# Two more seven-product tiles in the second group's feed-forward, with the first group's last sums done among them

## The chip, the cores and the metric

The kernel runs on one core of a Trainium2 chip. The metric is the device time of one execution in microseconds; the median of a few executions is given. The core has a matrix engine (TensorE, PE in the profile), a vector engine (VectorE, DVE), a scalar engine (ScalarE, ACT), a general engine (GpSimd, POOL), and a queue engine that only issues transfers (SyncE, SP).

## What is computed

One layer of a streaming encoder, for a prompt of 1024 frames and 32 frames of a running stream, with the same weights. The first half (three kinds of mixing heads, an output projection, a layer norm) is left out here, since the change doesn't touch it. The second half is a gated feed-forward with a residual and a layer norm:

```python
    mix = jnp.concatenate([...], axis=-1) @ w_o
    x = _layer_norm(ALPHA * x + (1 + g1) * mix, ln1_g, ln1_b)
    h = x * (1 + sc2) + sh2
    y = (jax.nn.silu(h @ w_gate) * (h @ w_up)) @ w_down
    x = _layer_norm(ALPHA * x + (1 + g2) * y, ln2_g, ln2_b)
```

The model width is 1024, the hidden width of the feed-forward 2816, that is 22 tiles of 128 columns.

## The kernel before

**Layout.** Activations lie with the feature on the partitions: 8 tiles (k) of 128 features by the frames. The 1056 frames are two groups: group 0 has 512 frames, group 1 has 544 (512 of the prompt's second half and the 32 others), worked on in two ranges of 272 columns. All matrix products are made in three matmuls of a rounded type, high part by high part, high by low and low by high (`gemm`, lines 130 to 132), so each operand is split first: ScalarE rounds it (the cast that makes `whi`, `ah`, `acth`), VectorE subtracts to get the rest (`wlo`, `al`, `actl`). For weights that is `weights` (lines 117 and 118).

**Order of the work around the change.** Group 0's feed-forward comes first. The 22 tiles j of gate and up weights are cut into six lists (`GROUPS`); after the tiles of a list and one more, `down` adds that list's share of the down projection into `z`. In the last list of group 0 (`g == WOB`) group 1's output projection and its first layer norm (`ln1`, phase `lna1`) are woven in. That norm writes group 1's modulated input `h` in two parts as the operand of the next products (`hh`, `hl`, lines 1240 and 1241) and also stores it to memory (`self.dh`, line 1239). Then comes the last `down` of group 0, whose evacuation (line 1212) is followed by `ln_sum` for group 0's second norm: a square on ScalarE (line 1073), a running sum of squares on VectorE (line 1074, `qs`) and a running sum on GpSimd (line 1083, `zs`), 16 pieces of 256 columns. `ln1_res(1)` turns group 1's normed rows into the residual of its second norm: 16 in-place scalings on GpSimd (line 1268). They must be done before group 1's first `down` adds to `z`.

**Group 1's tiles.** Tiles 0, 1 and 2 go by `up`: gate and up product, each for two ranges, each 8 k by 3 matmuls: 96 matmuls of 272 columns. From tile 3 (`SJ = 3`) on, `sup` makes the same 2 x 2 blocks (gate and up; first and second half of k; two ranges) by seven block products in the manner of Strassen and Winograd: 7 x 4 k x 3 = 84 matmuls. It needs sums of weight blocks and sums of operand blocks.

- The weights: per tile, three loads (gate weights, a part of the weight sums `self.dp[j]`, and 256 KB of the up weights called `w2`), then two adds on VectorE (lines 1387 and 1388) and splits of `w1`, `w3`, `w4` (128x1024 each) and `w2` (128x512) at lines 1381 and 1382. `self.dp[j]` is made in memory by `sums`: a copying transfer from SP's queue (line 1331) and an accumulating transfer from GpSimd's queue (line 1333), a few tiles ahead.
- The operand: `sup_operand` loads `h` from `self.dh`, k and k + 4 together, makes four sums of 272 columns (lines 1356 to 1359) and splits two rows of 544 (lines 1361 and 1362) into `self.T`, which lies where group 0's operand lay (`ah`, `al` of the pool `ph`). Four steps k. Its buffers hold two steps; the loads of the next two are issued after the step whose buffers they take.
- The products of a tile stand in the order: 1 and 2 on `w1` with the plain operand, 3 on `w3` with T's first part, 4 on `w4` with T, 5 on `w3` with the plain operand, 6 on `w4` and 7 on `w2` with T. Lines 1407 to 1411, 1418 and 1419 take them out of PSUM; lines 1413 to 1422 make the gated activation and split it.

The steps of the operand are issued while `up` of tiles 0 to 2 is written, behind the last activation (`lastact`). Behind every tile from 3 on, `turns` gives a number of steps of group 0's second norm (`ln2`, phase `lnb0`): first the mean and variance, then per k a subtraction (line 1465), a scaling (line 1481), an affine step on ScalarE (line 1483) and, for every second k, a store.

Each engine runs its instructions in one fixed order, which a planner makes from the order in which the program writes them and from estimated times; `issue_after` holds an instruction behind another one in that plan.

Of the kernel before, what the change touches and what calls it, by code (L numbers as in the profile page):

```python
# [7 lines left out]
F32 = mybir.dt.float32  # L8
# [7 lines left out]
P = 128  # L16
# [30 lines left out]
FF = 22  # L47
SJ = 3
TS = 1
# [19 lines left out]
class Kernel:  # L69
    def __init__(self, ctx, tc, d):  # L70
        self.ctx, self.tc, self.nc, self.d = ctx, tc, tc.nc, d
        self.n = 0
        self.phase = "start"

    def pool(self, name, bufs=1, ctx=None, **kw):
# [22 lines left out]
    def tie(self, ins, target, engines):  # L98
        for i in ins:
            if i.engine in engines and "DMA" not in type(i).__name__ and "Dma" not in type(i).__name__:  # L100
                self.tc.add_manual_dep(i, target.ins.name, mybir.DependencyInfo(
                    mybir.DependencyClass.NoSync, mybir.DependencyReason.SCHED_ONLY), reason="order")

    def weights(self, src, nk, ncol, eng=None, pool=None):
# [958 lines left out]
    def ln_sum(self, st, z, m, sl):  # L1063
# [5 lines left out]
        if st["last"] and m != o[7]:  # L1069
            sq = self.t((self.pg, self.pu)[m % 2], [P, 512], F32, self.utag[m % 2])[:, :sl.stop - sl.start]  # L1070
        else:
            sq = self.t(self.p2, [P, 272], F32, "tmp", 4)[:, :sl.stop - sl.start]
        nc.scalar.activation(sq, z[:, m, sl], AF.Square)
# [260 lines left out]

    def sup_operand(self, ks):

# [6 lines left out]
        def load(k):  # L1343
            self.phase = "sup"
            x, y = ((self.t(self.px, [P, 544], F32, z, 1) for z in ("c", "uv")) if k % 2 else
                    (f(self.t(self.px, [P, 544], F32R, z, 1)) for z in ("w2h", "w2l")))
            self.load(x, self.dh[:, k])
            self.load(y, self.dh[:, k + 4])
            return x, y

        loaded = {k: load(k) for k in ks[:2]}
        yield
        for k in ks:
# [6 lines left out]
            for z, (h, l) in zip((x, y), self.T):  # L1360
                nc.scalar.copy(h[:, k], z)
                tt(l[:, k], z, f(h[:, k]), ALU.subtract)
            if k + 2 in ks:
                loaded[k + 2] = load(k + 2)
            yield
# [218 lines left out]
    def run(self):  # L1584
# [164 lines left out]
        for g, (j0, nj) in enumerate(GROUPS):  # L1749
# [26 lines left out]
            for j in range(j0 + (g > 0), j0 + nj + (g < last)):  # L1776
                weave(self.up(0, j, act, pa, WIDE if 0 < j < GROUPS[-1][0] else MM[0]))
            if g == WOB - 1:
                st = self.ln_begin(nc.gpsimd, sum=False)
                self.down(0, g, act, WIDE, st)  # L1780
            else:
                self.down(0, g, act, WIDE)
        st.update(pivot=False, sum=True)
        self.down(0, last, act, MM[0], st)
        self.ln1_res(1)
        self.st0 = st
# [3 lines left out]
        self.px = self.pool("px")  # L1790
        operand = self.sup_operand(range(4))
        next(operand)
# [5 lines left out]
        norm0 = norm0()  # L1798
        turns = [1, 1, 2, 2, 2, 1] * 2
        for g, (j0, nj) in enumerate(GROUPS):  # L1800
            for j in range(j0 + (g > 0), min(j0 + nj + (g < last), FF - TS)):
                if self.nsum <= FF:
                    self.sums()
                if j >= SJ:
                    self.sup(j, act, pa)
                    with tc.issue_after(self.lastact.ins):
                        for _ in range(turns.pop(0) if turns else 0):
                            next(norm0, None)
                    continue
                for i, _ in enumerate(self.up(1, j, act, pa, MM[1])):  # L1810
                    if 0 < 2 * j + i // 2 < 5 and i % 2:
                        with tc.issue_after(self.lastact.ins):
                            next(operand, None)
            if g < last:
# [135 lines left out]
```

## Time and profile before

| what | us |
|---|---|
| median of 3 executions | 1334.85 |
| lowest, highest | 1334.41, 1336.23 |
| the profiled execution | 1335.24 |
| its span, first to last instruction | 1333.1 |

The profile is of one execution, so its own time, 1335.24, belongs to its rows; 2.1 us lie around the span. Engines are named PE, DVE, ACT, POOL and SP; PEld is the loading of weights into the matrix engine. A row of the timeline has the start, the time taken, engine, line of the kernel, operation, output <- inputs, shape, and in square brackets the idle time before it with what ended it. Tiles are named by the phase that made them, so a buffer taken over from an earlier phase can carry that one's name. Rows with "x14 | 9.2, 707" are groups: count, busy time in us, mean in ns.

### The profile page before, as it was taken

The page shows a single profiled execution, that of the slowest core. Times are in us where ns is not written, and L with a number is a line of the kernel's source. Part 1 is how long each engine was busy: PE and PEld are TensorE (multiplying, and loading weights), DVE is VectorE, ACT ScalarE, POOL GpSimd, SP SyncE. Part 2 cuts the span into 40 slices and gives each one's busy share as a digit, 9 for nine tenths or more (in the row PEclk, how much of TensorE's full clock was granted, in tenths as well). Part 3 has the DMA queues.
Part 4 walks back from the last instruction along what each step waited for, and adds up shares of the span by engine and source line. Part 5 has one row for each costly group of instructions (what it writes and reads, how often), then busy time and mean ns, then how long its engine had stood idle before and what let it go on. Part 6 is the DMA issues. An engine that isn't in the chain of part 4 may idle for free.

```text
span 1333.1 us, 24982 instructions
## 1 busy us (share of the span) xinstructions
PE 1318.8 (99%) x9426; PEld 1197.1 (90%) x9426; DVE 989.8 (74%) x2106; ACT 648.3 (49%) x1285; POOL 183.0 (14%) x219
## 2 busy tenths in 40 slices
PE   9999999999999999999999999999999999999996
PEld 6798888978999888888887888999999999999996
DVE  5636667667778677777776676778989997978677
ACT  3424446444437645455355354436664463635344
POOL 0102100011305000000000001134700000000523
PEclk9999999999999999999999999999999999999998
DMA  9775565533758755354343333663786866644311
GB/s 365 279 257 167 177 181 180 153 129 111 223 170 257 186 137 147 112 163 115 112 137 111 102 104 125 194 159 114 207 216 166 233 185 181 183 134 140 98 49 67
DMA packets 118119, 217.43 MB, mean 163 GB/s; under 512 B 18324, under 2 KB 62480, under 8 KB 118000
## 3 DMA queue, kind: packets, MB, share of 16 engines
q1 hardware_dynamic: 111184, 204.37, 48.8%
q0 software_dynamic: 5616, 10.86, 4.9%
q8 instruction: 74, 1.21, 0.4%
q10 hardware_dynamic: 1200, 0.62, 0.2%
q14 instruction: 45, 0.37, 0.1%
HBM read 184.95 MB, written 50.77 MB: 177 GB/s over the span
## 4 chain that ended last, share of the span: by engine, by line
PE 96%; DMA 1%; ACT 1%; SPq 0%; DVE 0%; issue 0%; ACTq 0%
PE up_g L132 6%; PE up_g L130 6%; PE up_g L131 6%; PE dn_g L132 4%; PE dn_g L130 4%; PE dn_g L131 4%; PE tm_g L404 4%; PE tm_g L406 3%; PE tm_g L405 3%; PE sup_u L132 3%; PE sup_u L131 3%; PE sup_u L130 3%; PE fox_t L938 2%; PE wo_g L130 2%; PE wo_g L132 2%; PE wo_g L131 2%
## 5 line engine op out<-in xcount | busy, mean ns | idle before, releaser
L131 PE MATMUL up_g<-ada_al,up_whi 128*128 128x512 f32 (+1 forms) x384 | 140.5, 366 | 0.0
L132 PE MATMUL up_g<-ada_ah,up_wlo 128*128 128x512 f32 (+1 forms) x384 | 140.3, 365 | 0.0
L130 PE MATMUL up_g<-ada_ah,up_whi 128*128 128x512 f32 (+1 forms) x384 | 140.1, 365 | 0.0
L1381 ACT CAST sup_whi<-sup_raw 128x1024 fp32r<-128x1024 f32 x54 | 56.6, 1051 | 96.7 <-PE dn_u L131 39.9
L117 ACT CAST up_whi<-up_raw 128x1024 fp32r<-128x1024 f32 x50 | 52.5, 1049 | 68.0 <-PE dn_g L131 35.8
L130 PEld LDWEIGHTS up_g<-ada_ah,up_whi 128*128 128x128 f32 x384 | 72.4, 189 | 11.5 <-issue 0.4
L131 PEld LDWEIGHTS up_g<-ada_al,up_whi 128*128 128x128 f32 x384 | 72.4, 189 | 11.0
L132 PEld LDWEIGHTS up_g<-ada_ah,up_wlo 128*128 128x128 f32 x384 | 72.5, 189 | 10.7
L1382 DVE TENSOR_TENSOR sup_wlo<-sup_raw,sup_whi 128x1024 fp32r<-128x1024 f32 x54 | 69.1, 1280 | 15.3 <-ACT sup_whi L1381 15.3
L1212 DVE SCALAR_TENSOR_TENSOR wo_z<-dn_g,start_mod,wo_z 128x512 f32<-128x512 f32 (+4 forms) x120 | 60.2, 521 | 22.7 <-PE dn_g L132 22.3
L911 ACT ACTIVATE fox_p<-fox_s,fox_fmx 128x384 f32<-128x384 f32 (+2 forms) x96 | 55.1, 578 | 45.1 <-DVE fox_fmx L909 25.4
L130 PE MATMUL dn_g<-up_acth,dn_whi 128*128 128x512 f32 (+2 forms) x200 | 73.7, 370 | 0.0
L132 PE MATMUL dn_g<-up_acth,dn_wlo 128*128 128x512 f32 (+2 forms) x200 | 73.7, 368 | 0.0
L131 PE MATMUL dn_g<-up_actl,dn_whi 128*128 128x512 f32 (+2 forms) x200 | 73.4, 368 | 0.0
L118 DVE TENSOR_TENSOR up_wlo<-up_raw,up_whi 128x1024 fp32r<-128x1024 f32 x50 | 64.6, 1293 | 8.6 <-ACT up_whi L117 7.7
L906 DVE TENSOR_REDUCE fox_fmx<-fox_s 128x1 f32<-128x384 f32 (+2 forms) x96 | 53.1, 554 | 21.1 <-PE fox_s L903 19.8
L117 ACT CAST dn_whi<-dn_raw 128x1024 fp32r<-128x1024 f32 (+1 forms) x44 | 42.7, 971 | 49.5 <-PE up_g L131 33.3
L943 ACT CAST fox_pth<-fox_t 128x512 fp32r<-128x512 f32 (+1 forms) x80 | 41.6, 542 | 43.1 <-PE fox_t L938 42.1
L118 DVE TENSOR_TENSOR dn_wlo<-dn_raw,dn_whi 128x1024 fp32r<-128x1024 f32 (+1 forms) x44 | 49.5, 1126 | 9.8 <-ACT dn_whi L117 9.7
L944 DVE TENSOR_TENSOR fox_ptl<-fox_t,fox_pth 128x512 fp32r<-128x512 f32 (+1 forms) x80 | 49.8, 632 | 7.0 <-ACT fox_pth L943 6.7
L1333 POOL DMA_DIRECT2D start_dp<-w_gu x19 | 19.7, 1039 | 226.0 <-DMA start_dp<-w_gu 226.0
L404 PE MATMUL tm_g<-tm_whi,start_ah 128*128 128x264 f32 (+2 forms) x160 | 49.9, 312 | 0.0
(694 smaller groups left out, 4680.6 us busy)
## 6 DMA issues: line engine op xcount, KB each, us to landing
up_raw<-w_gu SPq DMA_DIRECT2D x50, 512.0 KB
ada_late<-w_ada SPq DMA_DIRECT2D x28, 512.0 KB
dn_raw<-w_dn SPq DMA_DIRECT2D x28, 512.0 KB
sup_raw<-w_gu SPq DMA_DIRECT2D x20, 512.0 KB
start_dp<-w_gu SPq DMA_DIRECT2D x19, 512.0 KB
start_dp<-w_gu POOLq DMA_DIRECT2D x19, 512.0 KB, 8.6
wo_raw<-w_o SPq DMA_DIRECT2D x18, 512.0 KB
sup_raw<-start_dp SPq DMA_DIRECT2D x18, 512.0 KB
```

Of the source, the lines that this page charges most:

```text
L117: nc.scalar.copy(hi[:, :w], raw[:, :w])
L118: (eng or nc.vector).tensor_tensor(lo[:, :w], raw[:, :w], f(hi[:, :w]), ALU.subtract)
L130: nc.tensor.matmul(ps, hi, xh(k), start=start and k == 0, stop=False)
L131: nc.tensor.matmul(ps, hi, xl(k), start=False, stop=False)
L132: self.lastmm = nc.tensor.matmul(ps, lo, xh(k), start=False, stop=stop and k == n - 1)
L404: nc.tensor.matmul(ps[:, :ncol], xh, hi, start=k == 0, stop=False)
L906: nc.vector.tensor_reduce(mxs[:, x:x + 1], s[:, :w], AX.X, ALU.max, negate=True)
L911: nc.scalar.activation(pr[:, lo:hi], banks[x][:, :hi - lo], AF.Exp, bias=mxs[:, 0:1], accum_out=sums[:, x:x + 1])
L944: nc.vector.tensor_tensor(pl[:, :e], ps[:, :e], f(ph[:, :e]), ALU.subtract)
L1212: self.lastz = self.nc.vector.scalar_tensor_tensor(z[:, m, x:y], ps[:, x - a:y - a], g[i], z[:, m, x:y], ALU.mult, ALU.add)
L1381: nc.scalar.copy(h, x)
L1382: tt(l, x, f(h), ALU.subtract)
```

## The change

Group 1's tiles 1 and 2 go by `sup`, too (`SJ = 1`). So two more weight sums are made in memory: `sums` runs after tiles 17 and 18 of group 0 as well, and from there on makes the sums of the same tiles at the same places as before.

The operand T is thus needed after tile 0. All eight loads are issued at the start: step 2 and 3 are loaded into two of the five buffers of `acth` and `actl`. The four steps are written between the parts of tile 0, without being held behind the last activation.

`ln_sum` for group 0's second norm is no longer done in the last `down` but behind tiles 2, 3, 4 and 5, four pieces each (`SUMS`), ahead of the norm's turns; the square has a buffer of its own. `ln1_res(1)` is written after tile 0. All GpSimd instructions of both get a dependency on the last subtraction of the operand (`behind`). The turns of the norm stand behind the same tiles as before up to tile 8, then start again at tile 11.

```diff
-SJ = 3
+SJ = 1
+TURNS = (0, 0, 1, 1, 2, 2, 2, 1)
+SUMS = (0, 4, 4, 4, 4)
...
+    def behind(self, first):
+
+        for i in self.nc.cur_bb.bb.instructions[first:]:
+            if i.engine == mybir.EngineType.Pool:
+                self.tc.add_manual_dep(i, self.lastT.ins.name, mybir.DependencyInfo(
+                    mybir.DependencyClass.Sync, mybir.DependencyReason.DATA), reason="behind")
...
-            sq = self.t(self.p2, [P, 272], F32, "tmp", 4)[:, :sl.stop - sl.start]
+            pool, w, tag, n = (self.px, 256, "sq", 1) if st is self.st0 else (self.p2, 272, "tmp", 4)
+            sq = self.t(pool, [P, w], F32, tag, n)[:, :sl.stop - sl.start]
...
-            x, y = ((self.t(self.px, [P, 544], F32, z, 1) for z in ("c", "uv")) if k % 2 else
+            x, y = ((self.t(self.px, [P, 544], F32, z, 1) for z in ("c", "uv")) if k == 1 else
+                    (f(self.t(pool, [P, 544], F32R, z, 5)) for z in ("acth", "actl")) if k else
                     (f(self.t(self.px, [P, 544], F32R, z, 1)) for z in ("w2h", "w2l")))
...
-        loaded = {k: load(k) for k in ks[:2]}
+        loaded = {k: load(k) for k in ks}
...
-                tt(l[:, k], z, f(h[:, k]), ALU.subtract)
-            if k + 2 in ks:
-                loaded[k + 2] = load(k + 2)
+                self.lastT = tt(l[:, k], z, f(h[:, k]), ALU.subtract)
...
                 weave(self.up(0, j, act, pa, WIDE if 0 < j < GROUPS[-1][0] else MM[0]))
+                if j > GROUPS[-1][0] - 2:
+                    self.sums()
...
-        st.update(pivot=False, sum=True)
+        st.update(pivot=False)
         self.down(0, last, act, MM[0], st)
-        self.ln1_res(1)
         self.st0 = st
...
-        turns = [1, 1, 2, 2, 2, 1] * 2
+
+        def sum0():
+            for a, b in MM[0]:
+                for m in range(KT):
+                    self.phase = "dn0"
+                    first = len(nc.cur_bb.bb.instructions)
+                    self.ln_sum(self.st0, self.z[0], m, slice(a, b))
+                    self.behind(first)
+                    yield
+
+        sum0 = sum0()
+        sums = list(SUMS)
+        turns = list(TURNS) * 2
...
                     with tc.issue_after(self.lastact.ins):
+                        for _ in range(sums.pop(0) if sums else 0):
+                            next(sum0, None)
                         for _ in range(turns.pop(0) if turns else 0):
                             next(norm0, None)
...
                 for i, _ in enumerate(self.up(1, j, act, pa, MM[1])):
-                    if 0 < 2 * j + i // 2 < 5 and i % 2:
-                        with tc.issue_after(self.lastact.ins):
-                            next(operand, None)
+                    next(operand, None)
+                if j == 0:
+                    for _ in operand:
+                        pass
+                    first = len(nc.cur_bb.bb.instructions)
+                    self.ln1_res(1)
+                    self.behind(first)
```

More of the change, by code (lines that the diff above doesn't have):

```diff
@@ L73, in __init__ @@
         self.phase = "start"
+        self.st0 = None
     def pool(self, name, bufs=1, ctx=None, **kw):
@@ L1333, in sums, with sup_operand @@
             self.nc.gpsimd.dma_start(self.dp[i - 1], blocks(i - 1)[:, 0:4:3], accum_op=ALU.add)
-    def sup_operand(self, ks):
+    def sup_operand(self, ks, pool):
         nc = self.nc
@@ L1790, in run @@
         self.px = self.pool("px")
-        operand = self.sup_operand(range(4))
+        operand = self.sup_operand(range(4), pa)
         next(operand)
```

## The prediction

> **What bounds the kernel now.** I read the page first: engine shares, then the chain that ended last.
>
> ```profile
> span 1333.1 us, 24982 instructions
> PE 1318.8 (99%) x9426; PEld 1197.1 (90%) x9426; DVE 989.8 (74%) x2106; ACT 648.3 (49%) x1285; POOL 183.0 (14%) x219
> PE 96%; DMA 1%; ACT 1%; SPq 0%; DVE 0%; issue 0%; ACTq 0%
> ```
>
> TensorE is busy for 99% of the span and is 96% of the chain, so a matmul taken out is worth its pitch, as long as nothing else becomes late. The share of VectorE, 74%, is an average, so I read the stretch that the change touches. First the timeline of TensorE, at the first matmul of group 1's tiles 0, 1, 2, of tile 3 (the first by seven products), and of what follows it:
>
> ```profile
> 946.09 0.28 PE L130 MATMUL up_g<-wo_ah,up_whi 128*128 128x272 f32 x1
> 958.10 0.29 PE L130 MATMUL up_g<-wo_ah,up_whi 128*128 128x272 f32 x1
> 970.13 0.29 PE L130 MATMUL up_g<-wo_ah,up_whi 128*128 128x272 f32 x1
> 982.16 0.29 PE L130 MATMUL sup_u<-wo_ah,sup_whi 128*128 128x272 f32 x1
> 992.68 0.38 PE L1095 MATMUL lnb_t<-up_zs,start_onesm 128*128 128x256 f32 x1
> ```
>
> A plain tile takes 12.03 us (96 matmuls, 0.125 us each), a seven-product tile 10.52 us (84 matmuls). Then the windows view around it: the end of group 1's first norm; from there to the end of group 1's first down projection; tiles 4 to 6 with the second.
>
> ```profile
> core 0: us, PE busy (x) PEld busy (x) DVE busy (x) ACT busy (x) POOL busy (x), PEclk, DMA share, GB/s
> 928.33:952.22 23.89, 23.89 (x203) 23.89 (x201) 23.82 (x45) 13.88 (x31) 19.51 (x19) 1.00 0.52 156
> 952.22:1011.80 59.58, 59.58 (x473) 59.32 (x472) 54.72 (x106) 34.33 (x67) 9.77 (x12) 1.00 0.86 222
> 1011.80:1061.80 50.00, 50.00 (x402) 50.00 (x401) 45.60 (x88) 25.06 (x37) 4.10 (x4) 1.00 0.72 194
> ```
>
> TensorE never stops, but VectorE has 0.07 us, then 4.9 us, then 4.4 us to spare. It is the next bound, and the change gives it more to do.
>
> **The change part by part.**
>
> *Matmuls removed.* Two tiles lose 12 matmuls each: 2 x (12.03 - 10.52) = **3.0 us**, all on the path. This is the whole possible gain, and it is certain.
>
> *VectorE, per tile.* One run without gaps in the VectorE timeline gives the pitch (start to start) of each operation of a seven-product tile:
>
> ```profile
> 1021.67 0.72 DVE L1418 TENSOR_TENSOR sup_c<-sup_g,sup_uv 128x544 f32<-128x544 f32 x1
> 1022.30 1.22 DVE L1382 TENSOR_TENSOR sup_wlo<-sup_raw,sup_whi 128x1024 fp32r<-128x1024 f32 x1
> 1023.44 0.43 DVE L1419 TENSOR_TENSOR sup_c<-sup_u,sup_c 128x272 f32<-128x272 f32 x1
> ...
> 1029.04 0.72 DVE L1422 TENSOR_TENSOR sup_actl<-sup_c,sup_acth 128x544 fp32r<-128x544 f32 x1
> 1029.67 0.42 DVE L1465 TENSOR_TENSOR wo_z<-wo_z,up_zs 128x256 f32<-128x256 f32 x1
> 1030.05 0.44 DVE L1411 TENSOR_TENSOR sup_sil<-sup_u,sup_uv 128x272 f32<-128x272 f32 x1
> 1030.41 0.42 DVE L1481 TENSOR_TENSOR wo_z<-wo_z,up_pv 128x256 f32<-128x256 f32 x1
> ```
>
> From 1021.67 to 1029.67 stand 13 of a tile's 15 operations, 8.0 us; the third large split (1.14) and L1411 (0.36) make 9.5 us. A plain tile has two such splits and six 272-wide operations: 2 x 1.14 + 6 x 0.36 = 4.4 us. Two tiles add 2 x 5.1 = 10.2 us of VectorE.
>
> *VectorE, what is freed.* Three things move: the 16 residual scalings on GpSimd go behind the last operand subtraction; group 0's 16 squares (ScalarE), 14 adds on VectorE and 14 on GpSimd go behind tiles 2 to 5. Before, they share the time of the norm:
>
> ```profile
> 949.86 1.75 DVE L118 TENSOR_TENSOR up_wlo<-up_raw,up_whi 128x1024 fp32r<-128x1024 f32 x1
> 952.22 5.55 DVE L1074 TENSOR_TENSOR up_qs<-up_qs,dn_tmp 128x256 f32<-128x256 f32 x4
> L1074 DVE TENSOR_TENSOR up_qs<-up_qs,dn_tmp x14: 407/413/4331, 951.5 to 961.4; 128x256 f32<-128x256 f32 x14
> L1074 DVE TENSOR_TENSOR up_qs<-up_qs,dn_tmp 128x256 f32<-128x256 f32 x14 | 9.2, 707 | 0.0
> 953.13 1.22 POOL L1083 TENSOR_TENSOR up_zs<-up_zs,wo_z 128x256 f32<-128x256 f32 x1
> 955.66 1.15 POOL L1083 TENSOR_TENSOR up_zs<-up_zs,wo_z 128x256 f32<-128x256 f32 x1
> L1268 POOL TENSOR_SCALAR wo_z<-wo_z,start_colp 128x272 f32<-128x272 f32 x8 | 9.3, 1167 | 0.4 <-ACT lna_tmp L1236 0.4
> 944.95 0.47 DVE L1212 SCALAR_TENSOR_TENSOR wo_z<-dn_u,start_mod,wo_z 128x256 f32<-128x256 f32 x1
> 945.34 0.47 DVE L1212 SCALAR_TENSOR_TENSOR wo_z<-dn_g,start_mod,wo_z 128x256 f32<-128x256 f32 x1
> ```
>
> While GpSimd runs, a split takes 1.75 instead of 1.22 us, and one add of 0.41 us took 4.33 us, beside GpSimd operations that stand back to back around 953 to 957. Of the 45 VectorE instructions from 928.33 to 952.22, 4 are splits, 14 are L1212 (pitch 0.39), some 27 are 256 or 272 wide: 4.6 + 5.5 + 9.7 = 19.8 us of work in 23.9 us. So 4.1 us are lost there, and 3.9 us more in the one long add. Two GpSimd adds of the norm itself (L1233) stay, so I choose to count 3.0 us of the 4.1 as won: the norm's last subtraction ends at 949.2 instead of 952.2.
>
> *The sum for VectorE* up to the end of the first down projection, in place of 54.72 us: minus tile 1's evacuation (2.2) and tile 2's all (4.4), minus the adds (9.2, 0.4 of it before 952.22: 8.8), plus the 8 of them that come back behind tiles 2 and 3 (2.9), plus two tiles (19.0), minus the 2.3 us that fit into tile 1's old split slots: **58.9 us**. There are 949.2 to 1008.8 (1011.8 less 3.0), 59.6 us. Bounds of what that costs: nothing, since TensorE never waited at 23.82 of 23.89 us; or, if VectorE keeps half of its 4.9 us of idle time and the moved GpSimd work costs it 1.5 us again (the 4.1 us above, less the norm's own, cut to half), 58.9 + 2.4 + 1.5 - 59.6 = 3.2 us. I take the middle, **1.6 us**.
>
> *The operand (T).* It is now due in tile 1. One k in the VectorE timeline:
>
> ```profile
> 965.32 0.43 DVE L1356 TENSOR_TENSOR sup_w2l<-sup_w2l,sup_w2h 128x272 f32<-128x272 f32 x1
> 965.79 0.44 DVE L1357 TENSOR_TENSOR sup_w2h<-sup_w2h 128x272 f32<-128x272 f32 x1
> ...
> 967.10 0.43 DVE L1312 TENSOR_TENSOR up_sil<-up_g,up_sil 128x272 f32<-128x272 f32 x1
> 967.45 0.72 DVE L1362 TENSOR_TENSOR lna_al<-sup_w2h,lna_ah 128x544 fp32r<-128x544 f32 x1
> 968.09 0.72 DVE L1362 TENSOR_TENSOR lna_al<-sup_w2l,lna_ah 128x544 fp32r<-128x544 f32 x1
> 968.72 0.43 DVE L1313 TENSOR_TENSOR up_sil<-up_u,up_sil 128x272 f32<-128x272 f32 x1
> ```
>
> 3.4 us less the foreign L1312 (0.35) is 3.05 us; with other work in the gaps of the dependent ones (0.47 against 0.36) 2.7. Product 3 starts two products (3.0 us) after 958.1, and reaches its fourth k at 962.2. VectorE from 949.2: rest of the sum weights 1.8, operand 10.4 to 11.6 (four k's, the last subtraction not needed yet), one evacuation 1.1: 962.5 to 963.7, so 0.3 to 1.5 us late. This is the same lateness seen at its first place, not added to 1.6.
>
> *Waits added.* GpSimd's scalings wait for the last operand subtraction; behind them in its queue stand the accumulating DMA issues, whose sums are used several tiles later, and the adds. 16 x 1.17 = 18.7 us from 963.7 end at 982.4, and the first down projection, which reads them, starts after 990. The squares have one buffer, so ScalarE waits for each add, with weight casts behind it; at 34.33 of 59.58 us it has room.
>
> *DMAs.* Eight operand loads instead of four stand at the head of SP's queue, and wait for the norm's stores:
>
> ```profile
> 949.09 0.86 SPq L90 DMA_DIRECT2D start_dh<-lna_tmp  x2
> 952.28 0.42 ACT L1073 ACTIVATE dn_tmp<-wo_z 128x256 f32<-128x256 f32 x1 [2.16 <-DMA start_dh<-lna_tmp]
> 780.00:815.00 35.00, 35.00 (x228) 31.66 (x227) 24.14 (x48) 19.74 (x42) 0.00 (x0) 1.00 0.26 85
> ```
>
> A store lands about 3 us after its issue; a load of that length brings the last k at 956, in time. Two more weight sums (four DMAs of 512 KB) are issued earlier, where the DMA engines are 26% busy: nothing. Two more w2 loads, 0.5 MB at 222 GB/s, are 2.4 us of transfer in a stretch at 86%, used last in their tiles: nothing, or part of the 3.2.
>
> *Later.* Tiles 4 and 5 get 8 adds (2.9 us): 48.5 of 50 us, no wait. The norm's turns fall on the same tiles as before.
>
> **Sum:** 1335.24 (span 1333.1 and 2.1 around it) - 3.0 + 1.6 = 1333.84. That execution is 0.39 above the median shown, so against 1334.85 I say **1333.5 us**.
>
> **The rivals.**
> *Full gain.* VectorE packs as densely as from 928 to 952 and TensorE waits for nothing: 1334.85 - 3.0 = 1331.9. For it: no wait of TensorE anywhere in the stretch before. Against it: 99% of VectorE's time is asked for.
> *GpSimd collides again.* The moved 16 scalings and 14 adds meet the splits and sums of tiles 1 to 3, where VectorE has no slack, and cost what they cost before, 4.1 + 3.9 = 8.0 us: 1334.85 - 3.0 + 8.0 = 1339.9. It decides from 5.7 us of lost time on. For it: the 4.33 us add. Against it: the operand is kept clear of it, and the scalings spread.
> [...]
> *Operand loads late.* If store and load each took the 8.6 us that the accumulating DMAs take,
>
> ```profile
> start_dp<-w_gu POOLq DMA_DIRECT2D x19, 512.0 KB, 8.6
> ```
>
> the last k comes at 949.6 + 17.2 + 2.4 = 969.2, 7 us late: 1338.9.
> That the change doesn't do what it says can't be: the matmuls are gone, and the wait on GpSimd is written as a dependency.
>
> **How the numbers follow.** A measurement of this kernel can tell about 0.2%, 2.7 us, from no change: 1332.2 to 1337.5. Forecast (TensorE loses 0.4 to 5.6 us of 3.0): 0.57. Full gain: 0.24. Collision: 0.13. Loads: 0.06. So faster 0.24, same 0.57, slower 0.19. The range, 1331.6 to 1338.3, leaves out most of the collision and the loads; the forecast's own is 1332.2 to 1335.1 (1.6 replaced by 0.4 and 3.2).
>
> **What would show it.** Tiles 1 and 2 at 84 matmuls; first matmul of tile 3 at 979.2 plus what was lost. Right: a wait of TensorE of 0.3 to 1.5 us at product 3 of tile 1 on L1362, and VectorE over 97% busy from 949 to 1008. Wrong: VectorE idle there by over 3 us with no wait of TensorE (full gain), or VectorE operations of 1.7 us and more beside L1268 (collision), or L1356 of the last k waiting for a DMA after 958 (loads).

## The result, and the profile after

| | us | executions |
|---|---|---|
| before | 1334.63 (1334.03 to 1336.23) | 4 |
| after | 1349.18 (1347.92 to 1349.94) | 4 |
| ratio | 1.0104 (95%: 1.0092 to 1.0117) | |
| profiled execution after, its span | 1349.14, 1347.2 | 1 |

The change makes the kernel 1% slower, by 14.5 us. The prediction was 1333.5, no difference that can be measured, in a range of 1331.6 to 1338.3: the time lies 11 us above the range.

Lines of the changed file stand 10 to 12 further down: L130 is now L140, L1074 L1085, L1083 L1094, L1095 L1106, L1268 L1279, L1333 L1344, L1356 L1368, L1362 L1374, L1382 L1392. In the runs from e8 on, many stand 3 further still; e10 has the lines of before. First the page after: span, busy time, and the shares of the chain that ended last.

```profile
span 1347.2 us, 24929 instructions
PE 1320.5 (98%) x9402; PEld 1197.3 (89%) x9402; DVE 994.5 (74%) x2120; ACT 652.4 (48%) x1283; POOL 185.0 (14%) x221
PE 88%; DMA 4%; DVE 3%; POOL 2%; ACT 1%; issue 1%; SPq 0%; DVEq 0%; ACTq 0%; POOLq 0%
```

TensorE's share of the chain fell from 96% to 88%, and the chain now passes through DMA, VectorE and GpSimd: the end is set elsewhere for a while. Where, the waits of TensorE say (waiting instruction, what released it, total, times, longest):

```profile
PE lnb_t L1106 <- POOL up_zs L1094: 10.2, 1, 10.2
...
PE sup_u L141 <- DVE dn_al L1374: 1.1, 1, 1.1
PE wo_g L141 <- DVE up_al L1164: 0.7, 2, 0.4
...
PE sup_g L140 <- ACT sup_whi L1391: 0.4, 1, 0.4
```

None of these four stood in the profile before. One makes most of the loss: `lnb_t` at L1106, the matmul that takes the mean of group 0's second norm, waits 10.2 us for GpSimd's running sum `zs`. GpSimd's timeline there, and TensorE's row:

```profile
971.76 1.04 POOL L1344 DMA_DIRECT2D start_dp<-w_gu  x1 [10.17 <-DMA start_dp<-w_gu]
972.38 20.14 POOL L1279 TENSOR_SCALAR wo_z<-wo_z,start_colp 128x272 f32<-128x272 f32 x16
992.49 2.60 POOL L1094 TENSOR_TENSOR up_zs<-wo_z 128x256 f32<-128x256 f32 x2
995.06 10.04 POOL L1094 TENSOR_TENSOR up_zs<-up_zs,wo_z 128x256 f32<-128x256 f32 x12
```
```profile
1004.47 1.22 PE L1106 MATMUL lnb_t<-up_zs,start_onesm 128*128 128x256 f32 x2 [10.18 <-POOL up_zs L1094]
```

The 16 residual scalings wait for the last operand subtraction and start at 972.38. Behind them, in order, stand the 14 adds of `zs`: 20.14 + 2.60 + 10.04 us, to 1005. TensorE works in order too: the mean's matmuls stand right behind tile 3, which ends at 994.3, and the next product behind them; it is busy 0.00 of the 10.17 us from 994.30 to 1004.47. It waits for a sum that needs no hurry. The mean's matmul takes one half of 256 columns, seven of the 14 adds. But the first two adds, which read no `zs`, begin the two halves, so the halves are interleaved, and the wait ends only where the last add begins.

The stop costs more than its length. Windows around it (busy time of PE, PEld, DVE, ACT, POOL, then the granted clock, DMA share, GB/s):

```profile
994.00:1000.00 6.00, 0.29 (x3) 0.07 (x1) 6.00 (x8) 1.17 (x2) 6.00 (x6) 0.93 0.98 320
1000.00:1004.50 4.50, 0.03 (x1) 0.03 (x1) 0.83 (x2) 0.00 (x0) 4.50 (x8) 0.50 0.58 215
1004.50:1010.00 5.50, 5.50 (x24) 5.32 (x25) 0.72 (x1) 2.91 (x6) 3.66 (x4) 0.55 0.60 82
1010.00:1016.00 6.00, 6.00 (x50) 6.00 (x49) 4.71 (x11) 2.02 (x3) 0.00 (x0) 1.00 1.09 185
```

After the stop TensorE runs 5.5 us at a granted clock of 0.55 and only then at 1.00: 5.5 x 0.45 = 2.5 us of full clock are missing, and the section behind the stop is 1.7 us longer than before, though two of its four mean matmuls have moved out of it. In finer windows the clock is 1.00 until 999.0, some 5 us into the stop, 0.50 from 999.5 on, and 1.00 again from 1009.5, some 5 us behind the stop.

The rest is smaller. From the first matmul of each section in TensorE's timeline, before and after:

| section | before | after | difference |
|---|---|---|---|
| up to group 1's output projection | 850.15 | 850.51 | +0.36 |
| output projection | 49.03 | 50.40 | +1.37 |
| group 0's last tiles and down projection, with group 1's norm | 46.91 | 47.21 | +0.30 |
| tile 0 | 12.01 | 12.03 | +0.02 |
| tiles 1 to 3 | 34.58 | 34.14 | -0.44 (-3.01 of matmuls, +2.57) |
| stop at the mean | 0 | 10.18 | +10.18 |
| mean and first down projection | 19.12 | 20.79 | +1.67 |
| tiles 4 to 6 | 31.58 | 32.45 | +0.87 (matmuls of the norm moved here) |
| from there to the end of the span | 289.72 | 289.49 | -0.23 |

The sum is 14.10, the difference of the spans (1347.2 - 1333.1). The matmuls are gone, as forecast; the upstream 1.4 us come from transfers. SyncE's rows and GpSimd's after, then the windows before and after:

```profile
831.59 0.44 SPq L89 DMA_DIRECT2D sup_w<-w_gu  x1
832.07 0.60 SPq L93 DMA_DIRECT2D start_dp<-w_gu  x1
```
```profile
839.47 1.04 POOL L1344 DMA_DIRECT2D start_dp<-w_gu  x1 [0.64 <-DMA start_dp<-w_gu]
```
```profile
835.00:850.00 15.00, 15.00 (x112) 14.27 (x111) 10.33 (x18) 5.65 (x14) 3.06 (x3) 1.00 0.57 174
```
```profile
835.00:850.00 15.00, 15.00 (x110) 14.19 (x109) 9.55 (x15) 4.14 (x9) 4.38 (x4) 1.00 0.87 239
```

One weight sum more (a copy at 832, its accumulation at 839) lies beside the loads of group 1's mix and brings the DMA share from 0.57 to 0.87; the output projection then waits for its operand (`wo_g` in the waits). The difference in tiles 1 to 3 is 1.07 us at the operand and 0.4 at a weight split, with some more in pieces too short for the list of waits.

### The profile page after: what moved, and what is told of

The parts are those of the page before. It is cut to its first block, busy times and chain, and to the rows that moved or that the text cites. A ratio compares the mean times of both kernels' runs of the same rounds, so it can differ in the third digit from the quotient of the medians.

```text
span 1347.2 us, 24929 instructions
## 1 busy us (share of the span) xinstructions
PE 1320.5 (98%) x9402; PEld 1197.3 (89%) x9402; DVE 994.5 (74%) x2120; ACT 652.4 (48%) x1283; POOL 185.0 (14%) x221
## 4 chain that ended last, share of the span: by engine, by line
PE 88%; DMA 4%; DVE 3%; POOL 2%; ACT 1%; issue 1%; SPq 0%; DVEq 0%; ACTq 0%; POOLq 0%
PE up_g L142 6%; PE up_g L140 6%; PE up_g L141 6%; PE dn_g L142 4%; PE dn_g L140 4%; PE dn_g L141 4%; PE tm_g L414 3%; PE tm_g L416 3%; PE tm_g L415 3%; PE sup_u L142 3%; PE sup_u L141 3%; PE sup_u L140 3%; PE fox_t L948 2%; PE wo_g L141 2%; PE wo_g L142 2%; PE wo_g L140 2%
## 5 line engine op out<-in xcount | busy, mean ns | idle before, releaser
L140 PE MATMUL up_g<-ada_ah,up_whi 128*128 128x512 f32 (+1 forms) x384 | 140.1, 365 | 0.0
L1391 ACT CAST sup_whi<-sup_raw 128x1024 fp32r<-128x1024 f32 x60 | 62.4, 1049 | 87.1 <-PE dn_u L141 38.4
L1392 DVE TENSOR_TENSOR sup_wlo<-sup_raw,sup_whi 128x1024 fp32r<-128x1024 f32 x60 | 76.2, 1275 | 11.1 <-ACT sup_whi L1391 11.0
L140 PEld LDWEIGHTS up_g<-ada_ah,up_whi 128*128 128x128 f32 x384 | 72.4, 189 | 11.5 <-ACT fm_qkh L487 0.4
L127 ACT CAST up_whi<-up_raw 128x1024 fp32r<-128x1024 f32 x46 | 48.3, 1051 | 66.8 <-PE dn_g L141 35.8
L142 PE MATMUL dn_g<-up_acth,dn_wlo 128*128 128x512 f32 (+2 forms) x184 | 69.3, 377 | 0.0
L140 PE MATMUL dn_g<-up_acth,dn_whi 128*128 128x512 f32 (+2 forms) x184 | 69.0, 376 | 0.0
L141 PE MATMUL dn_g<-up_actl,dn_whi 128*128 128x512 f32 (+2 forms) x184 | 69.0, 376 | 0.0
L128 DVE TENSOR_TENSOR up_wlo<-up_raw,up_whi 128x1024 fp32r<-128x1024 f32 x46 | 59.3, 1289 | 9.1 <-ACT up_whi L127 8.1
L1344 POOL DMA_DIRECT2D start_dp<-w_gu x21 | 21.8, 1103 | 306.7 <-DMA start_dp<-w_gu 306.7
```

Of the source, the lines that this page charges most:

```text
L127: nc.scalar.copy(hi[:, :w], raw[:, :w])
L128: (eng or nc.vector).tensor_tensor(lo[:, :w], raw[:, :w], f(hi[:, :w]), ALU.subtract)
L140: nc.tensor.matmul(ps, hi, xh(k), start=start and k == 0, stop=False)
L141: nc.tensor.matmul(ps, hi, xl(k), start=False, stop=False)
L142: self.lastmm = nc.tensor.matmul(ps, lo, xh(k), start=False, stop=stop and k == n - 1)
L1391: nc.scalar.copy(h, x)
```

## The experiments

Four theories were tried. **A**: GpSimd's order makes the loss (mean behind adds behind scalings); take the wait and the slow clock behind it away, and some 1336.5 us are left. **B**: VectorE is too full, and the time is lost whatever stands on GpSimd. Two came up on the way. **C**: GpSimd's adds, once they run back to back, shut VectorE out. **D**: the additional weight sums delay group 1's output projection. Each run has its ratio to runs of the kernel before on the same chip; before lay at 1334.2 to 1335.6.

| run | tiles by seven from | median (lowest to highest), executions | ratio, 95% |
|---|---|---|---|
| e1 mean later | 1 | 1342.34 (1337.95 to 1349.80), 8 | 1.0057, 1.0034 to 1.0081 |
| e2 scalings early | 1 | 1341.08 (1339.25 to 1347.54), 7 | 1.0059, 1.0037 to 1.0080 |
| e3 seven alone | 1 | 1344.64 (1343.69 to 1345.85), 4 | 1.0068, 1.0051 to 1.0085 |
| e4 later alone | 3 | 1344.96 (1343.91 to 1345.58), 4 | 1.0072, 1.0057 to 1.0087 |
| e5 weight sums later | 1 | 1345.49 (1338.67 to 1348.85), 4 | 1.0079, 1.0050 to 1.0108 |
| e6 scalings on ScalarE | 1 | 1346.58 (1346.01 to 1348.29), 4 | 1.0096, 1.0081 to 1.0111 |
| e7 no GpSimd | 1 | 1338.93 (1338.10 to 1340.35), 6 | 1.0036, 1.0024 to 1.0049 |
| e8 spread | 1 | 1337.52 (1336.07 to 1338.70), 8 | 1.0024, 1.0013 to 1.0034 |
| e9 two with spread | 2 | 1336.13 (1334.34 to 1340.15), 11 | 1.0012, 1.0003 to 1.0020 |
| e10 two alone | 2 | 1337.24 (1336.50 to 1339.45), 11 | 1.0020, 1.0010 to 1.0029 |
| e11 two early | 2 | 1336.34 (1335.01 to 1339.31), 11 | 1.0013, 1.0004 to 1.0023 |
| e12 three early | 1 | 1337.90 (1335.37 to 1340.13), 9 | 1.0023, 1.0013 to 1.0033 |
| e13 two held | 2 | 1334.17 (1332.90 to 1335.79), 11 | 0.9996, 0.9987 to 1.0005 |
| e14 three held | 1 | 1343.99 (1343.01 to 1346.01), 5 | 1.0069, 1.0055 to 1.0083 |
| e15 three, not held | 1 | 1339.76 (1338.57 to 1343.08), 5 | 1.0042, 1.0028 to 1.0055 |

**e1, the mean later.** The norm's turns start one tile later, and its matmuls may not pass ahead of a tile's last matmul.

```diff
-TURNS = (0, 0, 1, 1, 2, 2, 2, 1)
+TURNS = (0, 0, 0, 1, 1, 2, 2, 2, 1)
...
-        turns = list(TURNS) * 2
+        turns = list(TURNS) + [1, 1, 2, 2, 2, 1]
...
+                            self.tie(nc.cur_bb.bb.instructions[first:], self.lastmm, (mybir.EngineType.PE,))
```

> The mean of group 0's second norm is written behind tile 4 instead of tile 3, and its matmul is held behind tile 4's last product on TensorE; all else is as in the changed kernel. Theory A (TensorE stops at that one matmul, for sums that stand behind 16 scalings on GpSimd): the wait of 10.2 us goes and with it the 2.5 us that the lowered clock took behind it, so 1349.2 - 12.7 = 1336.5, between 1335.5 and 1338. Theory B (VectorE can't supply two more seven-product tiles, and the one long wait only covers that): TensorE waits for VectorE or ScalarE in tiles 3 to 6 instead, 1341 or more.

The wait of 10.2 us is gone; no wait of TensorE behind the start is over 1.5 us. The fastest executions (1337.95, 1338.41) are near A, but the eight scatter over 12 us, and their mean granted clock falls with the time, 0.998 to 0.990. The profiled one, 1342.57, takes 51.04 us in the output projection and 15.45 in tile 1, and no VectorE operation there is over 1.5 us. A names the stop rightly and isn't all.

**e2, the scalings early.** `ln1_res(1)` goes back to its place in the kernel before, with no wait.

```diff
         self.down(0, last, act, MM[0], st)
+        self.ln1_res(1)
...
-                    self.ln1_res(1)
-                    self.behind(first)
```

> The 16 residual scalings on GpSimd go back to where they were before the change, without the wait for the operand; the 14 adds on GpSimd keep it. Theory A: the adds start at the last operand subtraction (about 972, or a few us later since the scalings now slow the norm's VectorE work) and need 12.6 us, so the sums are there at 985 to 989; the mean's matmul stands in tile 3 and waits 0 to 4 us: 1336 to 1341. Theory B: no change to speak of against the changed kernel, 1346 to 1350.

The wait at the mean shrinks to 0.3 us. The executions fall into two groups, 1339.25 to 1341.08 and 1347.20 to 1347.54. The same program differs by 6 to 8 us from one execution to another: something is left to chance.

**e3, the seven products alone.** The sums, squares and scalings stand as in the kernel before; only tiles 1 and 2 change.

```diff
-SUMS = (0, 4, 4, 4, 4)
+SUMS = ()
...
-        st.update(pivot=False)
+        st.update(pivot=False, sum=True)
         self.down(0, last, act, MM[0], st)
+        self.ln1_res(1)
```

> Tiles 1 and 2 by seven products alone: the sums, the squares and the scalings of group 0 stay in its last down projection, as before the change. Theory A: no long wait at the mean, since its sums are made early; 3.0 us of matmuls are gone, and the operand comes later than in the changed kernel, because GpSimd slows the norm (3 us) and the adds stand on VectorE ahead of it: TensorE waits 3 to 7 us for it in tile 1: 1334.6 - 3.0 + 3 to 7 = 1334.6 to 1338.6. Theory B: VectorE is fuller still than in the changed kernel, 1349 or more.

9 us over before, with no GpSimd work moved; 2.2 of it stand in the output projection (51.18). TensorE's waits and two windows:

```profile
PE sup_u L141 <- DVE lna_al L1374: 4.7, 2, 2.5
PE sup_u L140 <- DVE up_sil L1324: 2.0, 1, 2.0
```
```profile
970.00:976.00 6.00, 2.36 (x13) 2.14 (x14) 6.00 (x13) 3.14 (x7) 0.00 (x0) 0.75 0.28 85
976.00:982.00 6.00, 6.00 (x36) 6.00 (x36) 6.00 (x15) 0.96 (x4) 1.03 (x1) 0.68 0.42 122
```

With the sums in the way TensorE stops 6.7 us in tile 1, 4.7 of it at the operand, and the granted clock is 0.75 in 970 to 976 and 0.68 in 976 to 982; in e2, where only the sums are moved away, it stops 1.8 us. So moving the sums away was needed; moving them cost something else.

**e4, the moved sums alone.** Tiles 1 and 2 stay plain.

```diff
-SJ = 1
-TURNS = (0, 0, 1, 1, 2, 2, 2, 1)
-SUMS = (0, 4, 4, 4, 4)
+SJ = 3
+TURNS = (1, 1, 2, 2, 2, 1)
+SUMS = (8, 4, 4)
...
-                if j > GROUPS[-1][0] - 2:
-                    self.sums()
```

> The later sums and scalings alone: tiles 1 and 2 go by plain products as before the change (no weight sums for them), the operand is made in tile 0 with all its loads ahead, and 8 of the pieces stand before the norm's first turn behind tile 3, 4 and 4 behind tiles 4 and 5. Theory A: the same long wait though VectorE has 10 us less to do: scalings and adds need 20 + 13 us from the last operand subtraction, 965 to 970, so the mean's matmul, at about 993, waits 5 to 10 us, and the clock is lowered behind it for 1 to 3 us: 1341 to 1347. Theory B: VectorE has room, no wait: 1334 to 1336.

Also 9 us over before, and in A's range, but not by A's path: the wait at the mean is 2.4 us, not 5 to 10. 4.1 us are lost in tile 0 (16.07 us, before 12.01), where TensorE waits 2.48 us for a rest of the norm that stands in VectorE's order behind the operand's first load. And 1.5 us are a wait at the down projection, behind one long operation. VectorE's timeline, and GpSimd's beside it:

```profile
990.24 11.51 DVE L128 TENSOR_TENSOR dn_wlo<-dn_raw,dn_whi 128x768 fp32r<-128x768 f32 x1 [0.23 <-ACT dn_whi L127]
```
```profile
990.36 1.43 POOL L1094 TENSOR_TENSOR up_zs<-wo_z 128x256 f32<-128x256 f32 x2
991.74 7.62 POOL L1094 TENSOR_TENSOR up_zs<-up_zs,wo_z 128x256 f32<-128x256 f32 x11
999.31 0.83 POOL L1344 DMA_DIRECT2D start_dp<-w_gu  x1
999.91 1.00 POOL L1094 TENSOR_TENSOR up_zs<-up_zs,wo_z 128x256 f32<-128x256 f32 x1
```

A split of 128x768, 0.95 us elsewhere, takes 11.51 us, from the first of GpSimd's 14 adds to past the last one, with one DMA issue among them. That is C, though here little of it is on the path. The output projection takes 49.03 us, as before, with no additional weight sum: D.

**e5, the weight sums later.** e1, and the sums after tiles 17 and 18 are made where the first one is.

```diff
-                self.sums()
+                for _ in range(3):
+                    self.sums()
...
-                if j > GROUPS[-1][0] - 2:
-                    self.sums()
```

> The kernel of the run with the later mean, with one thing more: the two added weight sums are not started behind tiles 17 and 18 of group 0, but together with the first of the others, behind group 1's output projection. Theory D (the early transfers delay the loads of that projection): group 0's next products start at 899.2 to 899.6, as before the change, instead of 902.1; the fastest runs get 2 to 3 us faster, 1335 to 1336, the scatter of 12 us stays. If the early transfers are not the cause: start at 901 or later, and no gain.

Group 0's products resume at 900.28, between the two forecasts. That is 1.9 us before e1's 902.14, but 1.3 of it arise ahead of the output projection, which takes 50.52 us (e1 51.04, before 49.03). So the two early sums make at most 0.5 us of the delay: the copy at 831 and the DMA share of 0.83 in 835 to 850 are still there. The scatter of 10 us stays.

**e6, the scalings on ScalarE.** One letter, `RESE = "pp"` to `"pa"`, so that GpSimd has the adds alone.

> The changed kernel, with the 16 residual scalings on ScalarE instead of GpSimd. Theory A (queue on GpSimd): the 14 adds start at about 973 and are done by 986, the mean's matmul waits 0 to 4 us instead of 10.2, 1336 to 1340. Theory C (GpSimd's adds, back to back, shut VectorE out): the same, but one VectorE operation of 4 us or more stands beside the adds in tiles 1 to 3, and runs scatter by 4 us or more, 1338 to 1346.

By A this was to be the cure, since nothing stands ahead of the adds. The wait at the mean is gone, and in its place:

```profile
PE sup_g L142 <- DVE sup_wlo L1392: 8.8, 1, 8.8
```
```profile
975.33 11.44 DVE L1392 TENSOR_TENSOR sup_wlo<-sup_raw,sup_whi 128x1024 fp32r<-128x1024 f32 x1
```
```profile
975.68 1.90 POOL L1094 TENSOR_TENSOR up_zs<-wo_z 128x256 f32<-128x256 f32 x2
977.07 8.60 POOL L1094 TENSOR_TENSOR up_zs<-up_zs,wo_z 128x256 f32<-128x256 f32 x12
```

A split of 1.22 us takes 11.44 us, longer than all 14 adds together (10.5). C again, now on the path: tile 2 takes 22.50 us instead of 10.52. C had the long operation right; the scatter of 4 us or more that it forecast didn't come (2.3). In the profile of the change itself the adds met VectorE, too, but no split of 0.95 us there took more than 1.46; nor is a VectorE operation over 1.8 us beside the adds of e1, e2 and e5.

**e7, no GpSimd.** e6, and the 14 adds on VectorE as well, 0.41 us each.

```diff
-        st["eng"].tensor_tensor(...)
+        (nc.vector if st is self.st0 else st["eng"]).tensor_tensor(...)
```

> As the run with the scalings on ScalarE, and the 14 adds of the running sum are on VectorE too: GpSimd does no arithmetic in this stretch, VectorE has 5 us more. Theory C: no VectorE operation over 1.4 us in the stretch, runs within 2.5 us of each other, 1335 to 1338 (3.0 us of matmuls gone, about 2 us lost to the early weight sums and 2.5 us at the operand). Theory B (VectorE has too much to do): TensorE waits for VectorE in tiles 2 to 6, 1340 or more.

7.6 us faster than e6 with more work for VectorE; no split is long, and the six executions lie within 2.3 us. At 1338.93 it is 0.9 us above C's range, but below B's. B falls: VectorE has the room (57.18 of 59.60 us busy in 949.2 to 1008.8). C holds for e6.

**e8, spread.** e5 and e6 together, and each GpSimd add waits for VectorE's add of squares of the piece before, so that no two run back to back by design.

```diff
+        def add():
+            x = nc.vector.tensor_tensor(st["qs"][:, sl], st["qs"][:, sl], sq, ALU.add)
+            if st is self.st0:
+                self.lastT = x
```

> Scalings on ScalarE; each of the 14 adds on GpSimd waits for VectorE's add of the piece before, so that they can't stand back to back; weight sums behind the output projection; the mean held behind tile 4. Theories A, C and D together: no long wait, no VectorE operation over 2 us, start of the next products at 899.4; what stays is the late operand (2 to 4 us) against 3.0 us of matmuls: 1333.5 to 1336, runs within 2.5 us. Theory B: 1340 or more.

1337.52, within 2.6 us, 1.5 above the range expected. The large losses of the change are gone. It is still 3.3 us above before on the same chip (1334.19), though 3.0 us of matmuls are gone, so some 6 us are lost. The profile shows most of them: 1.9 in the output projection (50.89), 1.3 in group 0's down projection, 2.2 in tiles 1 to 3.

**e9 and e10, tile 2 alone.** e8 with `SJ = 2`; and the kernel before with `SJ = 2` and the operand's four steps in tiles 0 and 1. In both the weight sums and the norm's turns are shifted to match.

> The spread version (residual scalings on ScalarE, each GpSimd add behind a VectorE add, weight sums and mean later), but only tile 2 goes by seven products and tile 1 stays plain, so that the operand has a plain tile more. Matmuls: -1.5 us against before. If what the spread version still loses (5 to 6 us between 2.9 us slower than before and the 3.0 us of matmuls) comes from the operand being due one tile too early (its late sums at tile 1, and the clock after those waits), TensorE has no wait at tile 2 and the time is 1333.5 to 1335 with before at 1334.2. If it comes from the moved sums and the weight sums, the loss stays and the time is 1337.5 to 1339.

> The kernel before with tile 2 by seven products and nothing else moved: group 0's sums and the residual scalings where they were, one more weight sum, the operand's four steps in tiles 0 and 1. Matmuls: -1.5 us. If one tile less of room is still enough for the operand, 1333 to 1334.5 with before at 1334.2. If VectorE, which has 5 us of idle time in these 60 us, can't take 5.1 us more, a wait of TensorE of 1 to 3 us on the operand's splits at tile 2 and with the lowered clock behind it 1335.5 to 1338.

e9 lies between its two forecasts. From tile 0 to the end of the down projection it takes 63.10 us (before 65.71): 1.5 of matmuls and 1.1 of a moved mean are won and nothing is lost. What it loses stands upstream: the output projection takes 50.30, the down projection and what goes with it 47.98 (before 46.91), with VectorE waiting for casts behind the scalings on ScalarE. e10: 66.36 in the same stretch, so one more tile beside the unmoved sums costs more than it gives. But TensorE's waits at its operand are 0.8 us, below the 1 to 3 forecast, and more is lost upstream: its output projection takes 50.67 us.

**e11 and e12, scalings back on GpSimd, in their old place.** No wait on them; no weight sum written ahead of the output projection.

```diff
-RESE = "pa"
+RESE = "pp"
...
-                for _ in range(2):
-                    self.sums()
+                self.sums()
```

> As the run with tile 2 alone in the spread version, but the residual scalings are on GpSimd again and written where they stood before the change, with no wait, and no weight sum is added ahead of group 1's output projection (all are made one tile later instead). In that run the tiles themselves lost nothing (63.1 us from tile 0 to the end of the down projection, before 65.7); its losses were 1.3 us in group 1's output projection (50.30 us, before 49.03) and 1.1 us in group 0's last tiles and down projection (47.98, before 46.91), where VectorE waited for ScalarE with the scalings between its casts. If the weight sums and the scalings on ScalarE make these two, both go, and the time is 1333 to 1334 with before at 1334.9: the first version that is faster than before. If not, 1335.5 to 1336.5 again.

> The same with tiles 1 and 2 by seven products (all the matmuls of the change are gone, -3.0 us). The spread version with both tiles lost 1.9 us in the output projection, 1.3 us in group 0's down projection and 2.2 us in tiles 1 to 3, and ended 2.9 us above before. If the first two go and the last stays, 1334 to 1335 with before at 1334.9. If the operand, with the scalings out of ScalarE, also comes in time, 1332 to 1333. If the losses have other causes, 1336.5 to 1338.

The output projection takes 49.77 and 51.91 us, and the gain hoped for is missed in both. The copy still stands at 831: the planner put a sum that is written several tiles later right behind the load that it is held after, and that load, of up weights into a free buffer, is issued at 831. That also stands in the rows of the change above. And VectorE's timeline in e11 shows one more loss:

```profile
947.61 0.47 DVE L1226 SCALAR_TENSOR_TENSOR wo_z<-dn_u,start_mod,wo_z 128x256 f32<-128x256 f32 x1
953.74 0.44 DVE L1371 TENSOR_TENSOR sup_w2l<-sup_w2l,sup_w2h 128x272 f32<-128x272 f32 x1 [5.66 <-DMA sup_w2l<-start_dh]
```

VectorE sits 5.66 us on the operand's first load (as in e4, 4.15 us), with rests of the norm that tile 0 needs queued behind it; TensorE waits 1.3 us for one of them.

**e13 and e14, both held.** The up weights' load no longer counts as the load to hold a sum behind, and the operand steps are held behind the last activation (e14: three of them inside tile 0).

```diff
-        self.load(raw[2], self.d["w_gu"][j][:, 1536:])
+        nc.sync.dma_start(raw[2], self.d["w_gu"][j][:, 1536:])
...
-                    next(operand, None)
+                    if i % 2:
+                        with tc.issue_after(self.lastact.ins):
+                            next(operand, None)
```

> The last run with tile 2 alone, with two things mended that its profile and the last one's show. One: of the weight sums, one copy was issued at 831 us right behind an early load of up weights, and its accumulation at 838, beside the loads of group 1's mix (DMA share 0.84 in 835 to 850, before 0.57); here that copy is held behind the same tile's later load instead. Two: operand steps stood in VectorE's order ahead of the rests that tile 0 needs, and VectorE sat 5.7 us on their loads; here they are held behind the last activation, as before the change. If these two make the losses (0.7 us in the output projection, 1.3 us at tile 0), the output projection takes 49.0 us, TensorE doesn't stop in tile 0, and the time is 1333.3 to 1334.3 with before at 1334.8. If they don't, 1335.5 to 1336.5 again.

> The same with tiles 1 and 2 by seven products. The output projection loses 2.9 us in the run before this one and should lose nothing here. What is left is the operand, due 3 us into tile 1: its loads land at 954 to 959, so that a stop of 1 to 2 us there and some us at a lower clock stay. 1334 to 1335.5 with before at 1334.8. If the operand comes in time, 1332 to 1333; if the weight sum is not what delays the output projection, 1337 to 1338.

e13's output projection takes 49.03 us, TensorE doesn't stop in tile 0, and the time is in the range expected. Windows of e13, the one of the transfers and the one the prediction was about:

```profile
835.00:850.00 15.00, 15.00 (x112) 14.31 (x111) 10.31 (x19) 5.78 (x14) 2.91 (x3) 1.00 0.56 178
```
```profile
949.20:1008.80 59.60, 59.41 (x474) 59.19 (x473) 52.03 (x97) 31.13 (x55) 9.37 (x11) 1.00 0.74 205
```

It is the best version found: 0.9996 of before (0.9987 to 1.0005). Its profiled span is 1.2 us shorter, 1.5 of it matmuls, but the times can't be told from before. e14 missed by 8.5 us: the same edits with tile 1 stop TensorE 8.4 us at the operand.

**e15, the weight sum held, the operand not.**

> Tiles 1 and 2 by seven products as in e12, with the weight sum held as in e14 and the operand steps not held, as in the change. It tells the two edits of e14 apart. If the weight sum makes the 1.5 to 2.9 us that the output projection loses, and holding the operand made the 8 to 10 us stop in e14: output projection 49.0 us, operand wait of 1 to 2 us at tile 1, time 1334.5 to 1336 with before at 1334.7. If holding the weight sum (so that weights of tiles 1 and 2 come later or the operand's loads meet it) made the stop in e14, 1341 to 1344 again.

The output projection takes 49.03 us, and e15 differs from e12 (51.91) in that one line, so D is settled: the sum at 831 made that loss. The four runs without that copy (e4, e13, e14, e15) take 49.03 us there, the eleven with it 49.77 to 51.91. But the time is between the two forecasts. TensorE's stops in tile 1, three windows there, and VectorE's row on the operand's second load:

```profile
962.61 0.36 PE L140 MATMUL sup_u<-lna_ah,sup_whi 128*128 128x272 f32 x1 [1.77 <-DVE up_sil L1327]
964.90 0.59 PE L140 MATMUL sup_u<-lna_ah,sup_whi 128*128 128x272 f32 x1 [1.69 <-ACT lna_ah L1376]
967.00 0.60 PE L142 MATMUL sup_g<-lna_ah,sup_wlo 128*128 128x272 f32 x1 [1.04 <-DVE sup_wlo L1395]
```
```profile
961.00:964.00 3.00, 0.61 (x3) 0.42 (x3) 3.00 (x8) 2.50 (x5) 0.00 (x0) 1.00 0.94 360
964.00:967.00 3.00, 1.05 (x4) 0.73 (x4) 3.00 (x7) 3.00 (x7) 1.06 (x1) 0.51 0.35 30
967.00:970.00 3.00, 3.00 (x13) 3.00 (x14) 3.00 (x6) 1.08 (x3) 0.00 (x0) 0.50 0.91 156
```
```profile
959.98 0.44 DVE L1371 TENSOR_TENSOR sup_uv<-sup_uv,sup_c 128x272 f32<-128x272 f32 x1 [3.78 <-DMA sup_uv<-start_dh]
```

Tile 1 starts at 957.66, and the operand's second load lands at 960, with the third and fourth behind it: product 3 needs the fourth k some 4 us after the tile's start, and the sums and splits stand between. In the change, with the tiles 2.5 us later, the same row stood at 955.62. That load was issued at nearly the same time in both, so the lateness arises between its issue and its landing. The load in the change and in e15, and GpSimd's row in e15 just ahead of it:

```profile
951.86 0.32 SPq L89 DMA_DIRECT2D sup_uv<-start_dh  x1
```
```profile
950.77 1.06 POOL L1347 DMA_DIRECT2D start_dp<-w_gu  x1 [4.23 <-DVE wo_al L1255]
952.07 0.43 SPq L89 DMA_DIRECT2D sup_uv<-start_dh  x1
```

In e15 the accumulating transfer of a weight sum is issued 1.3 us ahead of the load; in the change there is none between 925 and 960. The DMA engines are busier, 1.06 in 955 to 962 against 0.80. The other runs agree: from the load's issue to the row that waited for it pass 7.7 to 7.9 us in e4, e14 and e15, which have an accumulation there, and 3.0 to 4.5 us in the change and e1, e2, e5 to e8, e11 and e12, which have none. So the weight sum that was held away from the output projection brings another one up to the operand. No run moved that accumulation alone, so this is read from the traces and not tested. With tile 1 by seven products, what is won upstream is given back at the operand.

## Why the prediction was wrong

- **Matmuls removed** (-3.0): right. Tiles 1 to 3 take three times 10.52 us plus stops, and in e13 two such tiles take 21.1.
- **VectorE, the sum** (1.6 us short): the place was right (tiles 1 to 3 lose 2.6), the cause wasn't. VectorE wasn't full but waiting: in 946 to 958 after it is busy 8.07 of 12 us, since it stands on the operand's stores and loads (2.23 and 1.71 us). The sign of being right, over 97% busy, was not met even ahead of the stop (41.13 of 45.10 us in 949.2 to 994.3). e7 gave it 5 us more and was the faster for it.
- **The operand (T)** (0.3 to 1.5 us late at product 3 of tile 1): measured 1.07, at the place named, on L1374. Its price was right partly by luck, because the tiles came 2 us late themselves. The rival "operand loads late" (0.06) didn't happen in the change, where no first subtraction waits for a load after 958. It did in e15: the stops in tile 1 are 4.5 us, and the granted clock is 0.51 and 0.50 from 964 to 970.
- **Waits added: the step that failed.** It named what is queued behind the 16 scalings, "the accumulating DMA issues, whose sums are used several tiles later, and the adds", and asked when the first down projection reads the scalings. It didn't ask who reads the adds: the mean's matmul, on an in-order TensorE, right behind tile 3. The rows on record were enough: 963.7 + 18.7 + 14 x 1.2 gives 999 against tile 3's end at about 991. TensorE stood 10.18 us there, and e1 takes that wait away. The scalings also started almost 9 us later than forecast, at 972.38, as the last split of the operand begins at 971.1.
- **The clock** had no term: 1.7 us more in the section behind the stop, whose first 5.5 us ran at a granted 0.55.
- **DMAs**, "where the DMA engines are 26% busy: nothing": wrong by 1.4 us. The sum that hurt isn't one of the two additional calls but one that the planner issued far ahead of its place.
- **GpSimd collides again** (8.0 us, 0.13): not in the change, whose VectorE has no operation over 1.5 us beside GpSimd's; the change lost its time in another way. In e6, where the adds hit a split on the path, the price is 12 us in one tile, above the rival's. The argument against it, that the operand is kept clear, was no argument about the adds. The add of 4.33 us in the rows of before is longer than its own 0.41 and any one GpSimd operation beside it (1.22): a run of them stands there.

So the loss of 14.1 us is 10.2 for the mean and 1.7 behind it, 1.4 for the weight sum, 2.6 in tiles 1 to 3 and 1.3 in the other rows of the table, less 3.0. A alone doesn't give the gain back: with the mean out of the way, C costs about as much in e6. What makes the longer executions of e1 and e2 is open, since their profiles show no such collision. The 1.3 us and the pieces of less than a microsecond in tiles 1 to 3 weren't taken apart.

## What to carry to other kernels

When a wait is put on one instruction of an in-order engine, list everything queued behind it, and for each of these the first reader on the engine that sets the end; here a mean nobody is in a hurry for stopped TensorE for 10.18 us, because its matmul stood in line. Work moved to "where there is room" brings its transfers and its collisions along (1.4 us upstream in the change, a split of 11.44 us in e6): look at where the planner really issues it. A gain of 3.0 us on a kernel at 99% is soon gone: the one stop of the change took its own 10.18 us and, estimated from 5.5 us at a granted 0.55, 2.5 us of clock behind it.

## What the runs showed of the hardware

- One VectorE split beside a run of 14 GpSimd adds lasted from about the first of them to past the last: 11.51 us for 0.95 (e4, with one DMA issue among the adds) and 11.44 for 1.22 (e6). With a dependency ahead of each add no split beside them took over 1.78 (e8) or 1.50 (e13). The same pair in the same kernel also passed each other (1.46 at most in the change). What decides it is open. The executions of e1, e2 and e5 scatter over 8 to 12 us and those of e7 and e8 over 2.6 at most, but e4 and e6, where a split lasts as long as the run, scatter over 1.7 and 2.3, and e9, with its adds apart, over 5.8. So the scatter isn't shown to come from this.
- The granted clock fell from 1.00 to 0.50 at about 964 in e15, though no stop there was over 1.77 us: TensorE was busy 0.61 of the 3.00 us from 961 to 964, in pieces.
- A load of the operand, 272 KB, took 7.7 to 7.9 us from its issue to its use in the three runs with an accumulating transfer issued 1.3 us ahead of it, and 3.0 to 4.5 us in the nine without.
